# A decoder block on one core: products of four up-projection steps made ahead and kept in DRAM, a gain row applied to results, weight sums in other stages, half of a transposition inside w_out

## Chip, cores and metric

The kernel runs on one core of a Trainium2 chip. The metric is the device time of one execution in microseconds (us); where several runs are given, the median counts. Every time of the kernel before that is quoted from a trace comes from one profiled execution.

## What is computed

Batch 1, 1024 tokens, model width 1024, feed-forward width 2816 (22 blocks of 128, called j), everything in float32. The part that the change touches comes after the two attention branches:

```
y = sigmoid(g_mla) * (o_mla @ w_o_mla) + sigmoid(g_fox) * (o_fox @ w_o_fox)   # "mix"
x = x + g_m * (y @ w_out)                                                     # "w_out"
h = rmsnorm(x, norm_ffn_g) * (1 + sc_f) + sh_f
u = h @ w_up                                                                  # "ffn_up"
gate, val = causal depthwise conv of width 3 over u, split in two halves
x = x + g_f * ((silu(gate) * val) @ w_down)                                   # "w_down"
return rmsnorm(x, norm_final_g)
```

`g_m`, `sc_f`, `sh_f`, `g_f` are rows of 1024 that are computed from a conditioning vector `c`.

## The kernel before

Each float32 product is made of three matmuls (`mm3`, lines 99 to 101): an operand is split into a high part (a copy to a shorter format, on ScalarE = ACT, line 80) and a low part (the difference, on VectorE = DVE, line 89, or on GpSimd = POOL, line 92). The usual matmul is 128x128 by 128x512.

A list scheduler decides the order of the instructions of each engine when the kernel is built; the engine then executes them in that order. All DMAs are issued by SyncE (SP), also in order: a DMA whose buffer is not free, or whose data is not made, holds back all that stand behind it. Pools with a number of buffers (`wr` has 2, `up`'s `u` has 6, PSUM's `mm` 5 and `sd` 3) decide how far loads run ahead.

The stages, with their place in the profiled execution:

- Projections and attention, to about 759 us.
- **mix** (759 to 850): a loop over eight blocks `d` of 128 columns, 48 matmuls each. For a block, 2 x 256 KB of weights (`wr`) and two gates of 512 KB (`o_raw`) are loaded. Behind the loop the conv weights are loaded and turned.
- **w_out** (853 to 963): output tiles of 128 tokens x 512 columns. Three groups of four tiles, each group over all eight k; a fourth group tile by tile. For each group 4 loads of 512 KB bring the weights into `wr`. POOL multiplies each 512 columns by the gain row `gm` (line 1129), then ACT and DVE split them into `wx_w`. Between groups one and two the rows `gf` and `sf` are made (`late_row`, lines 308 to 312). In group three the first four token blocks are normalised and turned by TensorE (`first_chunk`).
- **second chunk** (963 to 978): the last four token blocks t = 4 to 7 are turned; for each, DVE makes sums and differences and splits them (`t_N`, `t_T`, `t_B`).
- **ffn_up** (978 to 1422): w_up by Strassen-Winograd, 7 products of 12 matmuls for each j. Two of the products of j = 0 and 1 (B11, B21) are made ahead and stay in PSUM; the product that continues from B11 starts from a "seed", a PSUM copy made by ACT (line 1185). In the same loop `load_right` brings 22 blocks of w_down (512 KB each), and `sum_right` (lines 1294 to 1297) makes the four combinations N1, T2, N3, N4 of each pair, four DVE operations and four stores of 256 KB. `stored` makes four sums of each pair of activations on POOL.
- **w_down** (1422 to 1643): 7 products over 6 entries of the stored combinations, from a ring of 5 loads.

Of the kernel before, what the change touches and what calls it, by code (L numbers as in the profile page):

```python
# [13 lines left out]
ALU = mybir.AluOpType  # L14
# [15 lines left out]
RIGHT = ("N1", "N3", "T2", "N4")  # L30
# [40 lines left out]
class Block:  # L71
# [82 lines left out]
    def scratch(self):  # L154
        d = self.dram
        self.d_rope = d([2, P, S], F32, "rope")
        self.d_krope = d([32, 2, S], F32, "krope")
        self.d_qx = d([8, 4, S], F32, "qx")
        self.d_kx = d([8, 4, S], F32, "kx")
        self.d_mq = [d([P, 2, S], F32, f"mq{p}") for p in range(4)]  # L160
        self.d_mr = [d([P, 2, S], F32, f"mr{p}") for p in range(2)]
        self.d_mk = [d([P, 2, S], F32, f"mk{p}") for p in range(4)]
        self.d_v = [d([P, NT, 8, P], F32, f"v{b}") for b in range(2)]
        self.d_gate = [d([P, S], F32, f"gate{k}") for k in range(16)]
        self.d_o = [d([P, S], F32, f"o{k}") for k in range(8)]
# [3 lines left out]
        self.d_left = {n: [d([P, len(e), 512], F32, f"{n}{e[0]}") for e in ENTRIES] for n in LEFT}  # L169
        self.d_right = {n: [d([P, len(e), 512], F32, f"{n}{e[0]}") for e in ENTRIES] for n in RIGHT}  # L170
# [774 lines left out]


    def mix_and_up(self):
        nc, tc, a, ps = self.nc, self.tc, self.a, self.ps
        self.cwp = Pool(tc, "cw", "left")
        yp = Pool(tc, "y", "left")  # L950
        gm = yp([P, D], F32, "gm")
        y = [[yp([P, KD, 512], R32, f"y{c}{h}") for h in range(2)] for c in range(2)]
        op, oh, ol = self.op, self.oh, self.ol
        for d in range(KD):
# [28 lines left out]
        rows = self.wr([P, 1024], F32, "wr", 2)[: 2 * NJ, :512].rearrange("j (w p) -> j w p", w=4)  # L983
        self.dma(rows[:, 0:3, :], a["conv_w"][0].rearrange("w (j p) -> j w p", p=P))
        self.dma(rows[:, 3, :], a["conv_b"][0].rearrange("(j p) -> j p", p=P))
        self.cw = self.cwp([P, 4, 2 * NJ], F32, "cw")
        pt = ps([P, 512], F32, "mm", 5)
        for i in range(4):
            nc.tensor.transpose(pt[:, i * 44 : (i + 1) * 44], rows[:, i, :], self.ident[:44, :44])
        nc.vector.tensor_copy(self.cw, pt[:, :176].rearrange("p (w j) -> p w j", w=4))  # L990
# [9 lines left out]
        groups = [(half, slice(n * 512, (n + 1) * 512)) for half in range(2) for n in range(2)]  # L1000
        todo = [(g, k) for g in range(4) for k in range(0, KD, 2)]
        ahead = []

        def load():
            if todo:
                g, k = todo.pop(0)
                ns = groups[g][1]
                ahead.extend(self.scaled_rows(a["w_out"], k, ns, gm[:, ns], lambda: (lambda w: (w[:, 0:512], w[:, 512:1024]))(wx([P, 1024], R32, "w", 9))))

        def residual(x, acc, ns):  # L1010
            nc.vector.tensor_tensor(out=x[:, ns], in0=acc, in1=x[:, ns], op=ALU.add)

        def modulated(t, x):
# [6 lines left out]
            (nc.gpsimd if t in (1, 3, 5) else nc.vector).tensor_tensor(out=h, in0=h, in1=sf, op=ALU.add)  # L1020
# [17 lines left out]
        load()  # L1038
        hs, xs = [], []
        for g, (half, ns) in enumerate(groups[:3]):  # L1040
# [3 lines left out]
            acc = [ps([P, 512], F32, *(("sd", 3) if g != 1 and i < 3 else ("mm", 5))) for i in range(4)]  # L1044
            for k in range(KD):
                if k in (0, KD - 2):
                    held = []
                if k % 2 == 0:
                    load()
                held.append(ahead.pop(0))  # L1050
                if k in (0, KD - 2):
                    continue
                for i in range(4):
                    ts = slice(i * P, (i + 1) * P)
                    for e, (hi, lo) in enumerate(held, k + 1 - len(held)):
# [16 lines left out]
        for _ in range(3):  # L1072
            load()
# [35 lines left out]
        first = []  # L1109
        operands = [self.gate_operands(j) for j in range(2)]  # L1110
        for t in range(4, 8):
            second_chunk(t, hs[t])
        for j in range(2):
            x1 = ps([P, 512], F32, "mm", 5)
            self.product(x1, operands[j][1], "B11", True)
            first.append(([None] + operands[j][1:], x1, self.seed(x1, -1.0)))
        for j in range(2):
            self.product(first[j][1], operands[j][2], "B21", False)
        gx.close()
        self.ffn_up(first, tp)  # L1120

    def scaled_rows(self, w_dram, k, cols, gain, room):
# [4 lines left out]
        for i in range(2):  # L1127
            x = w[:, i, :]
            self.nc.gpsimd.tensor_tensor(out=x, in0=x, in1=gain, op=ALU.mult)  # L1129
            hi, lo = room()  # L1130
            self.hi_act(hi, x)
            self.lo_dve(lo, x, hi)
            out.append((hi, lo))
# [69 lines left out]
    def ffn_up(self, first, tp):  # L1203
# [13 lines left out]
        self.load_right(0)  # L1217
        ahead = self.operands(0, first[0][0])
        for j in range(NJ):
            a11, a12, a22, s1, s2, s3, s4 = ahead  # L1220
            if j + 1 < NJ:
                ahead = self.operands(j + 1, first[j + 1][0] if j + 1 < len(first) else self.gate_operands(j + 1))
            if j < len(first):
                _, x1, x6 = first[j]
            else:
                x1 = bank()
                self.product(x1, a11, "B11", True)
                x6 = self.seed(x1, -1.0)
# [5 lines left out]
            if j % 2 and j < NJ - 1:  # L1234
                self.load_right((j + 1) // 2)
            ug, uv = up([P, S], F32, "u", 6), up([P, S], F32, "u", 6)
            if j >= len(first):
                self.product(x1, a12, "B21", False)
            copied(x1, ug[:, lower])
# [15 lines left out]
            if j % 2 == 0:  # L1255
                self.sum_right(j // 2)
# [8 lines left out]
    def stored(self, j, act):  # L1265
# [7 lines left out]
        even, G = self.even, self.nc.gpsimd.tensor_tensor  # L1273
# [7 lines left out]
        for n, y in (("S1", x[:, lower]), ("S3", x[:, upper]), ("S2", even[:, lower]), ("S4", act[:, lower])):  # L1281
            self.dma(self.place(n, m), y)

    def load_right(self, m):

        self.pair = [self.upp([P, D], F32, f"dw{i}") for i in range(2)]
        for i, w in enumerate(self.pair):
            self.dma(w, self.a["w_down"][0, (2 * m + i) * P : (2 * m + i + 1) * P, :])

    def sum_right(self, m):  # L1290

        V, (x, z) = self.nc.vector.tensor_tensor, self.pair
# [29 lines left out]
    def down_raw(self, p, i):  # L1322
# [3 lines left out]
        x, w = (ring([P, 2, 512], F32, t, 5)[:, : len(e), :] for t in ("ar", "br"))  # L1326
        self.dma(x, self.d_left[left][i])
        if right in RIGHT:
            self.dma(w, self.d_right[right][i])
        else:  # L1330
            blocks = self.a["w_down"][0].rearrange("(m e p) n -> e p m n", e=2, p=P)
            self.dma(w, blocks[int(right[1]) - 1][:, e[0] : e[-1] + 1, HALVES[int(right[2]) - 1]])
        return x, w

    def down_split(self):

        out = []
        for src, c in zip(self.coming.pop(0), "ab"):
# [163 lines left out]
```

## Time and profile before

| | us |
|---|---|
| median of 3 runs | 1647.35 |
| the runs | 1647.15, 1647.35, 1649.14 |
| profiled execution | 1645.47 |
| its span, first to last instruction | 1643.5 |
| PE (TensorE) busy | 1557.2 |
| DVE busy | 1100.9 |

The profiled execution lies 1.88 us under the median, and 1.97 us of it lie outside the span. An engine's busy time is a sum over stages; where it waits is read stage by stage. The granted TensorE clock is a share of full speed: 1.00 is 2.4 GHz, 0.50 is 1.2 GHz.

### The profile page before, as it was taken

The page shows a single profiled execution, that of the slowest core. Times are in us where ns is not written, and L with a number is a line of the kernel's source. Part 1 is how long each engine was busy: PE and PEld are TensorE (multiplying, and loading weights), DVE is VectorE, ACT ScalarE, POOL GpSimd, SP SyncE. Part 2 cuts the span into 40 slices and gives each one's busy share as a digit, 9 for nine tenths or more (in the row PEclk, how much of TensorE's full clock was granted, in tenths as well). Part 3 has the DMA queues.
Part 4 walks back from the last instruction along what each step waited for, and adds up shares of the span by engine and source line. Part 5 has one row for each costly group of instructions (what it writes and reads, how often), then busy time and mean ns, then how long its engine had stood idle before and what let it go on. Part 6 is the DMA issues. An engine that isn't in the chain of part 4 may idle for free.

```text
span 1643.5 us, 21193 instructions
## 1 busy us (share of the span) xinstructions
PE 1557.2 (95%) x7574; PEld 1279.1 (78%) x7574; DVE 1100.9 (67%) x1726; ACT 776.8 (47%) x1341; POOL 430.6 (26%) x366
## 2 busy tenths in 40 slices
PE   7899979999997999999998979999999999999997
PEld 3778868888886888887876757777778888888886
DVE  5755666566554566575655789988898767746467
ACT  3434345544444455465533446544455455535445
POOL 1322025676770322301226431111111111101010
PEclk9999999999998999999999979999999999999999
DMA  8435497767455534516434525565653333587652
GB/s 289 143 103 173 154 256 190 219 185 203 138 157 138 127 96 116 126 55 218 156 128 161 172 77 179 193 198 198 199 167 109 109 116 108 180 327 244 201 182 103
DMA packets 191414, 270.84 MB, mean 165 GB/s; under 512 B 13026, under 2 KB 112034, under 8 KB 189966
## 3 DMA queue, kind: packets, MB, share of 16 engines
q1 hardware_dynamic: 191310, 269.50, 52.1%
q8 instruction: 59, 0.97, 0.2%
q14 instruction: 45, 0.37, 0.1%
HBM read 183.21 MB, written 73.67 MB: 156 GB/s over the span
## 4 chain that ended last, share of the span: by engine, by line
PE 37%; DVE 7%; DMA 5%; issue 4%; POOL 2%; ACT 1%; SPq 0%; DVEq 0%; POOLq 0%; ACTq 0%
PE ps_mm L99 5%; PE ps_mm L100 5%; PE ps_mm L101 5%; PE ps_sd L99 3%; PE ps_sd L100 3%; PE ps_sd L101 3%; PE ps_x L100 2%; PE ps_x L101 2%; PE ps_x L99 2%; DVE up_u L1201 2%; PE ps_y L101 2%; PE ps_y L99 2%; PE ps_y L100 2%; DMA up_dw<-in_w_down_dram 1%; POOL wr_wr L1129 1%
## 5 line engine op out<-in xcount | busy, mean ns | idle before, releaser
L99 PE MATMUL psA_fill<-hT_hi,ws_wh 128*128 128x512 f32 x352 | 150.0, 426 | 0.0
L92 POOL TENSOR_TENSOR ws_wl<-wr_wr,ws_wh 128x512 fp32r<-128x512 f32 x62 | 82.6, 1334 | 229.3 <-ACT ws_wh L80 206.4
L755 ACT ACTIVATE att_p<-psA_s,small_soft 128x128 f32<-128x128 f32 (+7 forms) x128 | 94.7, 740 | 100.1 <-DVE small_soft L749 98.5
L101 PE MATMUL psA_fill<-hT_hi,ws_wl 128*128 128x512 f32 x352 | 139.4, 396 | 0.0
L100 PE MATMUL psA_fill<-hT_lo,ws_wh 128*128 128x512 f32 x352 | 139.3, 396 | 0.0
L749 DVE TENSOR_REDUCE small_soft<-psA_s 128x1 f32<-128x128 f32 (+7 forms) x128 | 96.0, 751 | 52.2 <-PE psA_s L747 51.8
L745 PE MATMUL psA_s<-opn_k,opn_q 96*128 96x256 f32 (+7 forms) x480 | 115.2, 360 | 16.0 <-DMA opn_k<-opn_stg 8.8
L1201 DVE SCALAR_TENSOR_TENSOR up_u<-up_u,cw_cw,up_u 128x1023 f32<-128x1023 f32 x88 | 110.7, 1277 | 1.8 <-ACT up_u L1199 1.6
L745 PEld LDWEIGHTS psA_s<-opn_k,opn_q 96*128 96x128 f32 (+1 forms) x480 | 82.4, 193 | 25.4 <-issue 15.5
L89 DVE TENSOR_TENSOR ring_al<-ring_ar,ring_ah 128x1024 fp32r<-128x1024 f32 (+1 forms) x41 | 49.5, 1207 | 65.5 <-ACT ring_ah L80 65.5
L89 DVE TENSOR_TENSOR att_ptl<-psA_pt,att_pth 128x512 fp32r<-128x512 f32 x96 | 66.0, 688 | 35.8 <-ACT att_pth L80 35.4
L774 PE MATMUL psA_pt<-const_ident,att_p 128*128 128x128 f32 x576 | 86.6, 273 | 0.0
L757 DVE TENSOR_SCALAR att_p<-att_p,small_soft 128x128 f32<-128x128 f32 (+7 forms) x128 | 82.1, 642 | 4.1
L80 ACT ACTIVATE ring_ah<-ring_ar 128x1024 fp32r<-128x1024 f32 (+1 forms) x41 | 40.4, 985 | 86.0 <-PE ps_x L100 58.0
L101 PEld LDWEIGHTS psA_fill<-hT_hi,ws_wl 128*128 128x128 f32 x352 | 66.4, 189 | 15.7
L286 POOL TENSOR_TENSOR att_acc<-att_acc,att_lw 128x512 f32<-128x512 f32 x56 | 74.5, 1331 | 4.3
L1199 ACT ACTIVATE up_u<-up_u,cw_cw 128x1024 f32<-128x1024 f32 x44 | 54.7, 1243 | 43.4 <-DVE up_u L1243 42.3
L99 PEld LDWEIGHTS psA_fill<-hT_hi,ws_wh 128*128 128x128 f32 x352 | 67.4, 191 | 9.6
L100 PEld LDWEIGHTS psA_fill<-hT_lo,ws_wh 128*128 128x128 f32 x352 | 66.9, 190 | 9.7
L99 PE MATMUL ps_mm<-h_b,uw_gh 128*128 128x512 f32 x176 | 70.7, 402 | 3.0 <-DVE t_B L89 3.0
L100 PE MATMUL ps_mm<-h_b,uw_gh 128*128 128x512 f32 x176 | 70.7, 402 | 0.0
L101 PE MATMUL ps_mm<-h_b,uw_gl 128*128 128x512 f32 x176 | 70.6, 401 | 0.0
(432 smaller groups left out, 4533.4 us busy)
## 6 DMA issues: line engine op xcount, KB each, us to landing
wr_wr<-in_w_up_dram SPq DMA_DIRECT2D x46, 512.0 KB
att_lw<-in_w_ada_dram SPq DMA_DIRECT2D x64, 256.0 KB
wr_wr<-in_w_in_dram SPq DMA_DIRECT2D x28, 512.0 KB
up_dw<-in_w_down_dram SPq DMA_DIRECT2D x22, 512.0 KB
dram_S<-up_u SPq DMA_DIRECT2D x44, 256.0 KB
ring_ar<-dram_S SPq DMA_DIRECT2D x20, 512.0 KB
dram_N<-up_dw SPq DMA_DIRECT2D x33, 256.0 KB
dram_A<-up_u SPq DMA_DIRECT2D x33, 256.0 KB
```

The costliest lines, as they stand in the source:

```text
L89: self.nc.vector.tensor_tensor(out=out, in0=in_, in1=f32(hi), op=ALU.subtract)
L92: self.nc.gpsimd.tensor_tensor(out=out, in0=in_, in1=f32(hi), op=ALU.subtract)
L99: mm(ps, lhsT=lh, rhs=rh, start=start, stop=False, skip_group_check=onto)
L100: mm(ps, lhsT=lh, rhs=rl, start=False, stop=False, skip_group_check=onto)
L101: mm(ps, lhsT=ll, rhs=rh, start=False, stop=stop, skip_group_check=onto)
L286: nc.gpsimd.tensor_tensor(out=acc, in0=acc, in1=w, op=ALU.add)
L745: mm(o, lhsT=l, rhs=r[:, keys], start=n_ == 0, stop=diag is None and n_ == len(passes) - 1)
L749: nc.vector.tensor_reduce(out=st[:, 0:1], in_=view(s), axis=AX.X if i < 4 else AX.XY, op=ALU.max, negate=True)
L755: nc.scalar.activation(po, view(s), AF.Exp, bias=st[:, 0:1], accum_out=st[:, 1:2])
L757: nc.vector.tensor_scalar(out=pr, in0=pr, scalar1=st[:, 2:3], scalar2=None, op0=ALU.mult)
L774: nc.tensor.transpose(pt[:, n * 256 + e * P : n * 256 + (e + 1) * P], pr[:, kb * P : (kb + 1) * P], self.ident)
L1201: nc.vector.scalar_tensor_tensor(out=dst[:, back:], in0=u[:, : S - back], scalar=cw[:, tap, jj : jj + 1], in1=dst[:, back:], op0=ALU.mult, ...
```

## The change

RIGHT, the set of w_down combinations kept in DRAM, shrinks from four to two (N1, T2). They are summed inside the mix loop: 11 times a load of 512 KB and one of 256 KB, two DVE operations, two stores of 256 KB. N3 and N4 are formed in w_down from an extra load and one DVE subtraction (12 times). The conv weights move into the mix loop (d = 4). In w_out the 32 POOL multiplications by `gm` go; instead DVE multiplies each of the 16 result tiles in PSUM. The groups run (0,0), (0,1), (1,1), (1,0), so that group three reuses the split weights of group two: 12 loads and 24 splits instead of 16 and 32. The turning of blocks 4 and 5 is placed inside w_out's last tile. The two early products are made for four j instead of two; their results are copied by ACT, stored in DRAM (`d_early`, 8 stores of 256 KB) and loaded again (8 loads). In `stored` the sums of j < 8 go from POOL to DVE.

```diff
-RIGHT = ("N1", "N3", "T2", "N4")
+RIGHT = ("N1", "T2")
+EARLY = 4
...
+    def load_right(self, pool, m):
+        x, z = pool([P, D], F32, "dx", 2), pool([P, 512], F32, "dz", 2)
+        self.dma(x, self.a["w_down"][0, 2 * m * P : (2 * m + 1) * P, :])
+        self.dma(z, self.a["w_down"][0, (2 * m + 1) * P : (2 * m + 2) * P, 512:1024])
+        return m, x, z
...
+    def sum_right(self, pool, d):
...
+        for m, x, z in self.blocks:
+            V(out=x[:, lower], in0=x[:, lower], in1=x[:, upper], op=ALU.subtract)
+            V(out=z, in0=z, in1=x[:, lower], op=ALU.add)
+            self.dma(self.place("N1", m), x[:, lower])
+            self.dma(self.place("T2", m), z)
+        self.blocks = [self.load_right(pool, self.unsummed.pop(0)) for _ in range(2 if 0 < d < 5 else d < 7)]
...
+            if d == 4:
+                self.conv_weights()
+            self.sum_right(op, d)
...
-        groups = [(half, slice(n * 512, (n + 1) * 512)) for half in range(2) for n in range(2)]
-        todo = [(g, k) for g in range(4) for k in range(0, KD, 2)]
+        groups = [(half, HALVES[n]) for half, n in ((0, 0), (0, 1), (1, 1), (1, 0))]
+        todo = [(n, k) for n in (0, 1, 0) for k in range(0, KD, 2)]
...
         def residual(x, acc, ns):
+            nc.vector.tensor_tensor(out=acc, in0=acc, in1=gm[:, ns], op=ALU.mult)
             nc.vector.tensor_tensor(out=x[:, ns], in0=acc, in1=x[:, ns], op=ALU.add)
...
-                if g == 2 and k in (2, 3, 4, 5):
-                    first_chunk(k - 2, hs[k - 2])
+                if g == 2 and k in (3, 4, 5, 7):
+                    t = min(k - 3, 3)
+                    first_chunk(t, hs[t])
...
+        def early(j, left, right):
+            if right == "B11":
+                banks[j] = ps([P, 512], F32, "sd", 3)
+            self.product(banks[j], left, right, right == "B11")
+            x = gx([P, 512], F32, "e", 2)
+            nc.scalar.activation(x, banks[j], AF.Copy)
+            self.dma(self.d_early[j][:, int(right == "B21"), :], x)
...
+        with tc.high_priority(400):
+            second_chunk(4, hs[4])
+            second_chunk(5, hs[5])
...
-            self.nc.gpsimd.tensor_tensor(out=x, in0=x, in1=gain, op=ALU.mult)
...
+        def first_product(j):
+            if j < EARLY:
+                x = up([P, 512], F32, "p1", 2)
+                self.dma(x, self.d_early[j][:, 0, :])
+                return x
...
+            x6 = self.seed(x1, -1.0)
...
-            if j % 2 == 0:
-                self.sum_right(j // 2)
...
-        even, G = self.even, self.nc.gpsimd.tensor_tensor
+        even, G = self.even, (self.nc.vector if j < 8 else self.nc.gpsimd).tensor_tensor
...
+        if minus is not None:
+            self.nc.vector.tensor_tensor(out=w, in0=w, in1=minus, op=ALU.subtract)
```

The first place is SP's row in the mix: before, weights (`wr`) and gates only.

```order
405 L77 DMA o_raw_7910<-dram_gate_18_101 128x1024
406 L77 DMA o_raw_7913<-dram_gate_26_109 128x1024
407 L77 DMA wr_wr_8071<-in_w_o_mla_dram 128x4x128
408 L77 DMA wr_wr_8071<-in_w_o_fox_dram 128x4x128
409 L77 DMA wr_wr_8163<-in_w_o_mla_dram 128x4x128
410 L77 DMA o_raw_7978<-dram_acc_46_129 128x1024
411 L77 DMA wr_wr_8163<-in_w_o_fox_dram 128x4x128
```

In the changed kernel, at the same place, `dx` and `dz` are the blocks of w_down, `dram_N` and `dram_T` the stores of their sums.

```order
417 L79 DMA dram_T_108_191<-o_dz_7979 128x512
418 L79 DMA wr_wr_8095<-in_w_o_mla_dram 128x4x128
419 L79 DMA o_raw_8011<-dram_gate_19_102 128x1024
420 L79 DMA dram_row_130<-y_gm_7811 1x1024
421 L79 DMA o_raw_8014<-dram_gate_27_110 128x1024
422 L79 DMA dram_N_103_186<-o_dx_7982 128x512
423 L79 DMA dram_T_109_192<-o_dz_7983 128x512
424 L79 DMA o_dx_8087<-in_w_down_dram 128x1024
425 L79 DMA o_dz_8088<-in_w_down_dram 128x512
426 L79 DMA o_dx_8091<-in_w_down_dram 128x1024
427 L79 DMA o_dz_8092<-in_w_down_dram 128x512
428 L79 DMA wr_wr_8095<-in_w_o_fox_dram 128x4x128
```

The weights of block d = 3 (`wr_wr_8071` before, `wr_wr_8095` now) stood at places 407 and 408 and now stand at 418 and 428, with five blocks of sums loaded and three of them stored ahead of them.

The second place is ACT in w_out, where the row `sf` is made between the first and the second group; `wx_w` are high parts of w_out weights. Before:

```order
691 L80 ACTIVATE wx_w_8732<-wr_wr_8729 128x512
692 L80 ACTIVATE wx_w_8736<-wr_wr_8729 128x512
693 L80 ACTIVATE wx_w_8766<-wr_wr_8763 128x512
694 L80 ACTIVATE wx_w_8770<-wr_wr_8763 128x512
695 L312 ACTIVATE gx_sf_8500<-ps_mm_8671 128x512
696 L312 ACTIVATE gx_sf_8500<-ps_mm_8675 128x512
697 L80 ACTIVATE wx_w_8800<-wr_wr_8797 128x512
```

And now:

```order
692 L82 ACTIVATE wx_w_8782<-wr_wr_8777 128x512
693 L82 ACTIVATE wx_w_8811<-wr_wr_8809 128x512
694 L82 ACTIVATE wx_w_8814<-wr_wr_8809 128x512
695 L82 ACTIVATE wx_w_8979<-wr_wr_8977 128x512
696 L315 ACTIVATE gx_sf_8580<-ps_mm_8749 128x512
697 L315 ACTIVATE gx_sf_8580<-ps_mm_8753 128x512
698 L1047 ACTIVATE gx_h_8898,small_ss_8899<-gx_x_8757 128x1024
```

The splits still stand ahead of `gx_sf`, but no POOL operation stands ahead of the splits any more.

The third place is SP at the entry of ffn_up in the changed kernel; `gx_e` are copies of early products, `up_p` the loads from which the first two seeds are made. Before, neither existed.

```order
518 L79 DMA dram_early_100_183<-gx_e_9546 128x512
519 L79 DMA dram_early_101_184<-gx_e_9562 128x512
520 L79 DMA dram_early_100_183<-gx_e_9577 128x512
521 L79 DMA dram_early_101_184<-gx_e_9592 128x512
522 L79 DMA up_p_1_9624<-dram_early_98_181 128x512
523 L79 DMA up_p_2_9648<-dram_early_99_182 128x512
524 L79 DMA up_u_9681<-dram_early_98_181 128x512
```

The load of the first seed's data stands behind the store of the last early product.

## Rows read from the trace of the kernel before

**Rows 1.** The page: the span, and part 1 for TensorE (busy, share, instructions).
```profile
span 1643.5 us, 21193 instructions
PE 1557.2 (95%) x7574; PEld 1279.1 (78%) x7574; DVE 1100.9 (67%) x1726; ACT 776.8 (47%) x1341; POOL 430.6 (26%) x366
```

**Rows 2.** Windows: us, busy PE, PEld, DVE, ACT, POOL, clock, DMA share, GB/s.
```profile
1200.00:1225.00 25.00, 25.00 (x111) 20.42 (x110) 22.02 (x22) 12.17 (x15) 5.65 (x4) 1.00 0.63 211
1250.00:1275.00 25.00, 25.00 (x111) 20.42 (x110) 19.72 (x22) 13.07 (x16) 1.29 (x1) 1.00 0.30 91
1450.00:1475.00 25.00, 25.00 (x112) 20.68 (x111) 10.73 (x10) 11.05 (x14) 0.00 (x0) 1.00 0.95 357
```

**Rows 3.** What TensorE waited for, 849 to 1225 us: total, times, longest.
```profile
PE ps_mm L99 <- DVE gx_gf L310: 6.3, 1, 6.3
PE ps_sd L99 <- ACT ps_sd L1185: 5.6, 3, 2.1
PE ps_mm L1027 <- DVE t_B L89: 5.4, 1, 5.4
PE ps_sd L99 <- DVE up_u L1241: 3.9, 3, 1.7
PE ps_mm L1027 <- DVE gx_x L1101: 3.7, 1, 3.7
PE ps_mm L1027 <- DVE h_b L89: 3.5, 1, 3.5
PE ps_mm L99 <- DVE t_B L89: 3.0, 1, 3.0
PE ps_sd L99 <- ACT wx_w L80: 2.4, 1, 2.4
PE ps_sd L99 <- ACT uw_sh L80: 1.1, 1, 1.1
PE ps_sd L99 <- ACT up_c L1214: 0.8, 1, 0.8
PE ps_mm L99 <- ACT uw_sh L80: 0.8, 1, 0.8
```

**Rows 4.** Windows of 10 us in mix, w_out and the second chunk, same columns.
```profile
770.00:780.00 10.00, 10.00 (x46) 8.24 (x45) 7.60 (x11) 5.47 (x8) 1.91 (x2) 1.00 0.78 247
880.00:890.00 10.00, 5.32 (x18) 4.31 (x19) 6.63 (x7) 2.86 (x5) 7.07 (x6) 0.66 0.62 225
930.00:940.00 10.00, 9.39 (x38) 7.69 (x39) 8.28 (x13) 5.92 (x12) 2.54 (x2) 0.83 0.29 90
970.00:980.00 10.00, 3.85 (x12) 2.85 (x13) 10.00 (x15) 5.34 (x10) 3.20 (x3) 0.50 0.00 0
```

**Rows 5.** Timelines of POOL, ACT and DVE, 876 to 885 us: start, length, instruction.
```profile
876.71 5.85 POOL L1129 TENSOR_TENSOR wr_wr<-wr_wr,y_gm 128x512 f32<-128x512 f32 x4 [2.54 <-DMA wr_wr<-in_w_out_dram]
882.59 0.63 ACT L80 ACTIVATE wx_w<-wr_wr 128x512 fp32r<-128x512 f32 x1 [1.04 <-POOL wr_wr L1129]
883.12 1.06 ACT L312 ACTIVATE gx_sf<-ps_mm 128x512 f32<-128x512 f32 x2
883.86 1.28 DVE L310 SCALAR_TENSOR_TENSOR gx_gf<-ps_mm,gx_gf 128x512 f32<-128x512 f32 x2
```

**Rows 6.** SP's timeline in the mix, DMA of 755 to 850, POOL's weight splits.
```profile
763.96 5.86 SPq L77 DMA_DIRECT2D o_raw<-dram_gate  x4
DMA packets 8992, 15.06 MB, mean 158 GB/s; under 512 B 567, under 2 KB 5863, under 8 KB 8986
L92 POOL TENSOR_TENSOR ws_wl<-wr_wr,ws_wh 128x512 fp32r<-128x512 f32 x62 | 82.6, 1334 | 229.3 <-ACT ws_wh L80 206.4
```

**Rows 7.** The tile of w_down's sums: one operation (min/median/max ns), and why DVE idled.
```profile
L1296 DVE TENSOR_TENSOR up_dw<-up_dw,up_dw x11: 680/1668/1677, 996.9 to 1221.9; 128x512 f32<-128x512 f32 x11
  DMA up_dw<-in_w_down_dram: 12.9, 4
  issue: 9.1, 3
```

More of the change, by code (lines that the diff above doesn't have):

```diff
@@ L169, in scratch @@
         self.d_left = {n: [d([P, len(e), 512], F32, f"{n}{e[0]}") for e in ENTRIES] for n in LEFT}
+        self.d_early = [d([P, 2, 512], F32, f"early{j}") for j in range(EARLY)]
         self.d_right = {n: [d([P, len(e), 512], F32, f"{n}{e[0]}") for e in ENTRIES] for n in RIGHT}
@@ L950, in mix_and_up @@
         yp = Pool(tc, "y", "left")
+        y = [[yp([P, KD, 512], R32, f"y{c}{h}") for h in range(2)] for c in range(2)]
         gm = yp([P, D], F32, "gm")
-        y = [[yp([P, KD, 512], R32, f"y{c}{h}") for h in range(2)] for c in range(2)]
         op, oh, ol = self.op, self.oh, self.ol
+        self.blocks, self.unsummed = [], list(range(NJ // 2))
         for d in range(KD):
@@ L1036, in first_chunk @@
                 self.lo_dve(b1[1][sl], v, b1[0][sl])
-        load()
+        for _ in range(2):
+            load()
         hs, xs = [], []
@@ L1044, in mix_and_up @@
             acc = [ps([P, 512], F32, *(("sd", 3) if g != 1 and i < 3 else ("mm", 5))) for i in range(4)]
+            weights = []
             for k in range(KD):
-                if k in (0, KD - 2):
-                    held = []
-                if k % 2 == 0:
+                if k % 2 == 0 and g < 2 and (g, k) < (1, 4):
                     load()
-                held.append(ahead.pop(0))
+                weights.append((kept if g == 2 else ahead).pop(0))
                 if k in (0, KD - 2):
                     continue
+                first = k - 1 if k in (1, KD - 1) else k
                 for i in range(4):
                     ts = slice(i * P, (i + 1) * P)
-                    for e, (hi, lo) in enumerate(held, k + 1 - len(held)):
-                        self.mm3(acc[i], y[half][0][:, e, ts], y[half][1][:, e, ts], hi, lo, e == 0, e == KD - 1)
-                held = []
-                if g == 2 and k in (2, 3, 4, 5):
-                    first_chunk(k - 2, hs[k - 2])
+                    for e in range(first, k + 1):
+                        self.mm3(acc[i], y[half][0][:, e, ts], y[half][1][:, e, ts], *weights[e], e == 0, e == KD - 1)
+                if g == 2 and k % 2:
+                    load()
+                if g == 2 and k in (3, 4, 5, 7):
+                    t = min(k - 3, 3)
+                    first_chunk(t, hs[t])
+            kept = weights
             if g == 0:
@@ L1107, in second_chunk, with split_rows @@
                 (self.lo_pool if n == "N4" else self.lo_dve)(lo, v[n], hi)
[L1109 to L1112, printed above, removed]
+        def early(j, left, right):
[5 more added lines that the diff above has]
+            self.dma(self.d_early[j][:, int(right == "B21"), :], x)
+        banks = {}
+        gates = [self.gate_operands(j) for j in range(2)]
+        with tc.high_priority(400):
+            second_chunk(4, hs[4])
+            second_chunk(5, hs[5])
         for j in range(2):
-            x1 = ps([P, 512], F32, "mm", 5)
-            self.product(x1, operands[j][1], "B11", True)
-            first.append(([None] + operands[j][1:], x1, self.seed(x1, -1.0)))
+            early(j, gates[j][1], "B11")
+        second_chunk(6, hs[6])
         for j in range(2):
-            self.product(first[j][1], operands[j][2], "B21", False)
+            early(j, gates[j][2], "B21")
+        gates += [self.gate_operands(j) for j in range(2, EARLY)]
+        second_chunk(7, hs[7])
+        for j in range(2, EARLY):
+            early(j, gates[j][1], "B11")
+        for j in range(2, EARLY):
+            early(j, gates[j][2], "B21")
         gx.close()
-        self.ffn_up(first, tp)
-    def scaled_rows(self, w_dram, k, cols, gain, room):
+        self.ffn_up(tp)
+    def split_rows(self, w_dram, k, cols, room):
         w = self.wr([P, 1024], F32, "wr", 2).rearrange("p (i n) -> p i n", i=2)
@@ L1233, in ffn_up @@
             t = copied(x6)
-            if j % 2 and j < NJ - 1:
-                self.load_right((j + 1) // 2)
             ug, uv = up([P, S], F32, "u", 6), up([P, S], F32, "u", 6)
-            if j >= len(first):
+            if j < EARLY:
+                self.dma(ug[:, lower], self.d_early[j][:, 1, :])
+            else:
                 self.product(x1, a12, "B21", False)
-            copied(x1, ug[:, lower])
+                copied(x1, ug[:, lower])
             self.product(x6, s3, "N3", False)
```

85 lines of the change are left out of this document (39 added, 46 removed).

## The prediction, made before the changed kernel ran

> **What bounds the kernel now.** I read the page first: TensorE is busy for 1557.2 of 1643.5 us [rows 1], so a change that leaves the count of matmuls as it is (the order has 6763 rows on PE before and 6764 after) can save at most some 86 us of idle time, plus what the lower clock costs. Next, the 25-us windows: where TensorE never waits it does 111 or 112 matmuls in 25 us, 0.223 us each [rows 2]. Then what TensorE waited for between the mix and the middle of ffn_up [rows 3]: eleven kinds of wait, 36.5 us in all. Six of them lie in w_out and the turning of the second chunk (2.4 + 6.3 + 3.5 + 3.7 + 5.4 + 3.0 = 24.3 us), the others (12.2 us) at the entry of ffn_up and in its first half. In the mix it does not wait: 10.00 us busy in 770 to 780 [rows 4], and so it goes on in that stage; in w_down there is hardly a wait either (25.00 of 25 in 1450 to 1475 [rows 2]). So the change can win in w_out, the second chunk and ffn_up's first half, and it can lose in the mix, to which it moves work, and in w_down.
>
> After a wait the clock is lower: 0.66, 0.83 and 0.50 as means over the three 10-us windows that hold the waits for `gx_gf`, `h_b` and the second chunk [rows 4]. These are mixes of the levels 2.4 and 1.2 GHz: 0.66 is 6.8 us of ten at the lower one. If these lay last in the wait and first behind it, some 2.7 us fell on work behind the first wait and cost half of it, 1.3 us; by the same way 1.5 us behind the second.
>
> **The mix (loss).** 11 blocks x (512 + 256 KB loaded, 2 x 256 KB stored) are 14.4 MB, beside 15.06 MB that moved there before, at 158 GB/s on average [rows 6]. The 22 DVE operations of about 0.68 us (the shortest of `up_dw` [rows 7]) are 15 us in a stage where DVE is busy for 7.6 of 10 us at its fullest [rows 4], which is room enough over 91 us. The danger is SP: block d = 3's weights now stand behind five blocks of sums, d = 4's behind more. Counting the sizes of SP's new row from the first gate load (issued at 764 us [rows 6]), 9.7 MB lie up to and with d = 3's weights, 14.4 up to d = 4's, 18.7 to d = 5's, 22.1 to d = 6's. TensorE needs them at 793, 805, 816 and 827 us (the stage's 759 to 850 in eight equal blocks), about 3 us after landing: two splits on POOL of 1.33 each [rows 6]. With a rate r the lateness for d = 5 is 764 + 18.7 MB / r + 3 - 816. The highest rate in the trace is 357 GB/s at a DMA share of 0.95 [rows 2], 376 at a full share; 770 to 780 us had 247 at 0.78 [rows 4], 317 at a full share. At 376 d = 5 is 1 us late, at 340 6, at 300 13. I take 340, between the best row and the nearest scaled one: **+6 us**, with bounds 0 and +13.
>
> By the Trainium skill (HBM Reference, Specifications) a core that streams alone reaches about 425 GB/s. No run here shows it: the trace's best is 357. By that page the term would be 0, and the case would be the second rival's below.
>
> **w_out (gain).** The 6.3 us go to `gf` and `sf` [rows 3]. The timelines show why [rows 5]: POOL multiplies four tiles in 5.85 us after 2.54 us of waiting for a load, ACT splits the last at 882.59, only then turns to `gx_sf` (883.12), and DVE to `gx_gf` (883.86). ACT's order keeps splits ahead of `gx_sf` in the changed kernel, but these wait for loads alone; two loads are ahead instead of one. With 1.46 us of POOL per tile gone, I let TensorE resume about 0.6 us after its own last matmul for that row: 6.3 - 0.6 + 1.3 of clock is **-7 us**. The 3.5 us wait for `h_b` was DVE held up by weight splits and long operations beside POOL; in the new order group three needs no new splits and the turns come one k later. The gain is 3.5 + 1.5 of clock; I keep 1 us of it as a rest, **-4 us**. The first wait (2.4, ACT busy with the end of the mix) stays. DVE gets 16 products of about 0.7 us and loses 8 splits of the same length: +5.5 us, in a stage where it is not full. Bounds for w_out: -12 (both waits and their clocks gone) and -4 (the wait for `gf` only halved).
>
> **Second chunk and entry of ffn_up (even).** Before, 12.1 us of waits and about 2 us of lower clock. In 970 to 980 us DVE is busy for all 10 us [rows 4]: it is the limit there, with four blocks of sums and splits, and these stay. Turning two of them inside the last w_out tile saves perhaps 2.5 us, since the other two still wait for the residual and the norm. The next 48 matmuls made early are 10.7 us [rows 2], in which DVE prepares ffn_up's operands. But the first seed now comes from DRAM: last copy on ACT, store, load behind it on SP, then the seed. A load for which POOL waited took over 2.54 us [rows 5]; store and load one after the other are some 5 us, from the end of the early products, against 1.9 us of entry waits before [rows 3]. -2.5 + 3.1 is about 0: **0 us**, bounds -4 and +5.
>
> **ffn_up (gain).** Of its 12.2 us of waits 1.9 are the entry's, which leaves 10.3 [rows 3], on `ps_sd` seeds (ACT) and `up_u` (DVE). They come behind stretches where DVE stood still in front of `up_dw`: 12.9 us for w_down's loads and 9.1 by issue [rows 7]; DVE is in order, so all of ffn_up's own work stands behind it. With the sums gone these stop; 1200 to 1225 has DVE at 22.0 of 25 us with the sums, and 1250 to 1275, without them, at 19.7 with no wait on TensorE [rows 2]. Against that: j = 0 to 3 have five products, 60 matmuls or 13.4 us, and DVE needs at most 14.7 there: per j its row has seven operations on 512 columns, seven on 1024, and four sums of `stored` for every second j, at 0.64 us for 512 columns back to back (1.28 for two [rows 5]). DVE lags by up to 1.3 us per j, 5 in all, of which the buffers take some: I keep 4 us of waits. **-6.3 us**, bounds -9 and -2. `stored`'s sums on DVE last only to j = 7.
>
> **w_down (nothing).** 12 subtractions of about 1.3 us (twice 0.64) and 5.8 MB more. In 1450 to 1475 DMA is at 0.95, but the extra loads belong to products five to seven, later, and DVE is busy for 10.7 of 25 us there [rows 2]. Hidden by the ring's lookahead; without that cover, up to +3.
>
> **Sum.** +6 - 7 - 4 + 0 - 6.3 + 0 = -11.3 us on the profiled execution's 1645.47: 1634.2. The median of the runs lies 1.9 above it, so 1636.0 us.
>
> **Rivals.**
>
> *The mix starves (slower).* SP's queue is in order, and the new `dx` loads wait for their buffers' stores, so the stream stops and starts, as the mean of 158 GB/s shows it doing now [rows 6]. It decides when the mix loses 20.6 us, that is, by 17.3 us of other gains and the 3.3 us of the 0.2%: 18.7 MB in 816 + 20.6 - 767 = 69.6 us, a sustained 269 GB/s. For it: 247 in 770 to 780 [rows 4]. Against it: that window's share was 0.78, with SP's loads not wanted sooner. Time: at 250 GB/s d = 5 is 26 us late, 1656 us. Chance 0.17.
>
> *The mix hides everything (faster still).* At 376 GB/s or more the term is 0 to 1 and the entry wait overlaps: 1636 - 5 - 3 = 1628 us. For it: the highest row; against it: stores and loads wait for one another. Chance 0.19.
>
> *The waits only move (no change).* The `gf` and `sf` row stays behind splits whose loads come late, and DVE, with 16 more products in w_out and sums of `stored`, gives up half of ffn_up's gain: -3.5 - 2 - 3 + 6 = -2.5, 1645 us. For it: ACT's row keeps four splits ahead of `sf`; DVE is near full in the first half of ffn_up [rows 2]. Against it: DVE's idle time there is blocked time, not lack of work [rows 7]. Chance 0.14.
>
> The forecast itself: 0.50, with its own range 1630 to 1643.
>
> **Numbers.** 0.2% is 3.3 us, about what a measurement tells from no change; 1644.1 to 1650.6 counts as the same. Faster: 0.50 + 0.19 = 0.69, of which 0.01 goes to the upper edge: 0.68. Same: 0.14 and that 0.01: 0.15. Slower: 0.17. The range leaves out half of the starving case and the edge of the fast one: 1625 to 1652.
>
> **What would show it.** Mix: TensorE waits for `wr` splits at d = 3 to 6, 5 to 7 us in all, with the DMA share over 0.9 between 764 and 820 us. w_out: no wait over 2 us for `gx_gf`, none for `h_b`, clock at 1.00 there. Second chunk: waits for `t_B` or `uw_gl`, then one of about 5 us for the seed from DRAM. ffn_up: no idle DVE in front of loads, about 4 us of waits in j = 0 to 4, none behind j = 8. w_down: no new wait. It is wrong if the mix is longer than 101 us, if the seeds on ACT, which run ahead in order and wait for the `p1` loads, hold up the copies that free PSUM, or if DVE's lag in j = 0 to 3 is paid in full.

## The result, and the profile after

| | before | changed |
|---|---|---|
| median of 4 runs, us | 1647.25 | 1630.41 |
| lowest and highest | 1644.00 to 1649.14 | 1626.37 to 1634.27 |
| profiled execution | 1645.47 | 1631.67 |
| its span | 1643.5 | 1629.9 |

The ratio is 0.990, with a 95% interval of 0.987 to 0.9929: the change is faster by 12 to 21 us. Forecast were 11.3 us and a median of 1636.0, with a range of 1630 to 1643; the measured median lies 0.4 us inside the range's lower end. The two profiled executions differ by 13.8 us, and the stages are compared on them. The page after, against [rows 1]:

```profile
span 1629.9 us, 21135 instructions
...
PE 1552.7 (95%) x7574; PEld 1274.8 (78%) x7574; DVE 1086.5 (67%) x1741; ACT 776.4 (48%) x1337; POOL 356.8 (22%) x317
```

What TensorE waited for in the changed kernel, 745 to 1225 us, against [rows 3] (total us, times, longest):

```profile
PE ps_mm L311 <- ACT o_raw L82: 7.0, 2, 5.6
PE ps_sd L103 <- DVE uw_gl L91: 4.3, 1, 4.3
PE ps_mm L1057 <- DVE gx_h L1050: 2.8, 2, 2.5
PE ps_sd L101 <- ACT wx_w L82: 2.7, 1, 2.7
PE ps_sd L101 <- ACT uw_sh L82: 2.5, 1, 2.5
PE ps_mm L101 <- ACT uw_sh L82: 2.2, 1, 2.2
PE ps_mm L1057 <- DVE t_B L91: 1.8, 1, 1.8
PE ps_mm L103 <- DVE uw_sl L91: 0.7, 1, 0.7
PE ps_mm L102 <- DVE o_ol L91: 0.5, 1, 0.5
PE ps_sd L101 <- ACT ws_wh L82: 0.5, 1, 0.5
PE ps_sd L101 <- ACT up_c L1259: 0.4, 1, 0.4
PE ps_sd L103 <- POOL ws_wl L94: 0.4, 1, 0.4
PE ps_sd L101 <- DVE up_u L1293: 0.4, 1, 0.4
...
```

The waits for `gx_gf` (6.3) and `h_b` (3.5) are gone, and of the 10.3 us in ffn_up the last rows of this list are left, 1.5 us (`uw_sl`, `up_c`, `up_u`). At the head stands a wait that the kernel before does not have: TensorE at line 311, the matmuls of a late row, in the mix. The clock and the stages are read in 10-us windows (columns as in [rows 2]; the first three lie in the mix, then w_out's `gf`/`sf` place, then the second chunk):

```profile
770.00:780.00 10.00, 10.00 (x46) 8.26 (x45) 9.23 (x15) 5.12 (x7) 1.77 (x2) 1.00 0.84 299
...
800.00:810.00 10.00, 7.71 (x32) 5.42 (x30) 5.76 (x10) 3.38 (x4) 1.27 (x1) 1.00 0.92 330
810.00:820.00 10.00, 5.78 (x16) 4.19 (x17) 4.34 (x6) 5.83 (x8) 3.03 (x2) 0.66 0.96 337
...
880.00:890.00 10.00, 9.83 (x44) 7.81 (x43) 7.47 (x13) 4.32 (x8) 0.00 (x0) 1.00 0.50 164
...
960.00:970.00 10.00, 3.74 (x14) 2.22 (x12) 9.66 (x14) 8.32 (x14) 3.53 (x3) 0.83 0.01 2
970.00:980.00 10.00, 7.60 (x27) 6.12 (x28) 10.00 (x17) 5.45 (x10) 4.97 (x3) 0.83 0.58 184
```

880 to 890, where [rows 4] had 5.32 us of TensorE at a clock of 0.66, now has 9.83 at 1.00. In exchange 810 to 820 lies at 0.66 with DMA at 0.96 of its time.

Where a stage begins is read from the rows of the tiles, the first start of a group of matmuls:

```profile
L101 PE MATMUL ps_mm<-o_oh,ws_wh x64: 387/389/628, 759.3 to 858.3; 128*128 128x512 f32 x64
...
L103 PE MATMUL ps_mm<-wx_w,y_y x80: 388/389/398, 869.3 to 959.9; 128*128 128x512 f32 x80
L101 PE MATMUL ps_sd<-wx_w,y_y x48: 389/389/499, 864.5 to 933.0; 128*128 128x512 f32 x48
...
L101 PE MATMUL ps_sd<-t_T,uw_sh x88: 389/389/793, 1001.8 to 1396.8; 128*128 128x512 f32 x88
...
L101 PE MATMUL ps_x<-uw_gh x8: 389/389/389, 1408.5 to 1413.2; 128*128 128x512 f32 x8
```

The mix runs from the first row's first start to the third's, w_out from there to the second's last start, the turning with the early products to the fourth's first start (the first seeded product), ffn_up to the fifth's, w_down to the span's end. The same rows in every run give this table (us):

| kernel | mix | w_out | turn, early | ffn_up | w_down | median | ratio, 95% interval |
|---|---|---|---|---|---|---|---|
| before | 93.8 | 107.4 | 34.3 | 427.6 | 221.4 | 1647.25 | |
| changed | 105.2 | 95.4 | 41.9 | 406.7 | 221.4 | 1630.41 | 0.990 (0.987 to 0.9929) |
| changed, again (e11) | 106.8 | 96.6 | 42.8 | 407.0 | 221.4 | 1632.14 | 0.9908 (0.9888 to 0.9929) |
| e1 row later | 106.5 | 96.5 | 42.9 | 407.2 | 221.4 | 1633.33 | 0.9915 (0.9896 to 0.9935) |
| e2 sums in ffn_up | 95.4 | 96.6 | 44.7 | 410.1 | 221.3 | 1626.53 | 0.9876 (0.9854 to 0.9899) |
| e3 POOL scales | 107.9 | 104.2 | 42.0 | 407.0 | 221.6 | 1638.64 | 0.9965 (0.995 to 0.9979) |
| e4 two j early | 105.7 | 96.6 | 36.5 | 415.5 | 221.6 | 1634.25 | 0.9922 (0.9904 to 0.9939) |
| e5 `stored` on POOL | 109.5 | 95.0 | 42.3 | 408.4 | 221.4 | 1637.67 | 0.9949 (0.993 to 0.9968) |
| e6 turn behind w_out | 105.8 | 94.1 | 46.2 | 407.0 | 221.4 | 1631.56 | 0.9916 (0.9886 to 0.9947) |
| e7 paced sums | 95.5 | 95.0 | 43.6 | 407.1 | 221.4 | 1623.57 | 0.986 (0.9835 to 0.9885) |
| e8 before, two sums | 94.3 | 108.9 | 34.2 | 423.5 | 221.3 | 1641.28 | 0.9972 (0.996 to 0.9983) |
| e9 four buffers | 112.3 | 96.5 | 43.0 | 407.1 | 221.4 | 1639.97 | 0.997 (0.9956 to 0.9984) |
| e10 paced, six early | 96.3 | 96.6 | 55.0 | 397.5 | 221.9 | 1628.29 | 0.9888 (0.9873 to 0.9904) |

Two columns belong together: of two more j made early, 48 matmuls (10.7 us) go from ffn_up to the column before it. The changed kernel and its repetition show how far a stage differs by itself: 1.6 us in the mix, 1.2 in w_out, 0.9 in the turning, 0.3 in ffn_up. The mix of all kernels that sum 11 blocks in it with two buffers lies between 105.2 and 109.5, and the changed kernel's profiled execution has the shortest of these. Differences of an experiment are therefore given against both executions of the changed kernel where it matters. Where the mix begins differs too, from 754.3 to 760.7 us, in stages that no edit touches; this is why stages are compared, and not spans.

Against before the changed kernel's profiled execution stands thus: mix +11.4, w_out -12.0, turning and early products +7.6 less 10.7 = -3.1, ffn_up -20.9 plus 10.7 = -10.2, w_down 0. Each of these rests on one profiled execution of either kernel; with e11 in its place the first three are +13.0, -10.8 and -2.2.

### The profile page after: what moved, and what is told of

Same layout as the page of the kernel before. It is cut to its first block, busy times and chain, and to the rows that moved or that the text cites. A ratio compares the mean times of both kernels' runs of the same rounds, so it can differ in the third digit from the quotient of the medians.

```text
span 1629.9 us, 21135 instructions
## 1 busy us (share of the span) xinstructions
PE 1552.7 (95%) x7574; PEld 1274.8 (78%) x7574; DVE 1086.5 (67%) x1741; ACT 776.4 (48%) x1337; POOL 356.8 (22%) x317
## 4 chain that ended last, share of the span: by engine, by line
PE 43%; DVE 4%; DMA 4%; ACT 2%; issue 1%; SPq 0%; ACTq 0%; DVEq 0%
PE ps_mm L101 5%; PE ps_mm L103 5%; PE ps_mm L102 5%; PE ps_sd L101 4%; PE ps_sd L103 4%; PE ps_sd L102 4%; PE ps_x L102 2%; PE ps_x L103 2%; PE ps_x L101 2%; PE ps_y L102 2%; PE ps_y L101 2%; PE ps_y L103 2%; DMA wr_wr<-in_w_up_dram 1%; DVE up_u L1246 1%; DMA o_raw<-dram_acc 1%
## 5 line engine op out<-in xcount | busy, mean ns | idle before, releaser
L760 DVE TENSOR_SCALAR att_p<-att_p,small_soft 128x128 f32<-128x128 f32 (+7 forms) x128 | 86.1, 672 | 4.1
L82 ACT ACTIVATE uw_sh<-uw_s 128x1024 fp32r<-128x1024 f32 x44 | 46.7, 1062 | 61.8 <-PE ps_mm L102 29.2
L91 DVE TENSOR_TENSOR uw_gl<-wr_wr,uw_gh 128x1024 fp32r<-128x1024 f32 x24 | 29.5, 1232 | 65.9 <-ACT uw_gh L82 64.4
L1328 POOL TENSOR_TENSOR up_u<-up_u 128x512 f32<-128x512 f32 x7 | 9.0, 1288 | 263.9 <-DVE up_u L1306 263.9
L82 ACT ACTIVATE att_pth<-psA_pt 128x512 fp32r<-128x512 f32 x96 | 57.2, 595 | 19.8 <-PE psA_pt L777 16.2
```

The lines of the kernel that those rows point to most:

```text
L82: self.nc.scalar.activation(out, in_, AF.Copy, scale=scale)
L91: self.nc.vector.tensor_tensor(out=out, in0=in_, in1=f32(hi), op=ALU.subtract)
L760: nc.vector.tensor_scalar(out=pr, in0=pr, scalar1=st[:, 2:3], scalar2=None, op0=ALU.mult)
```

## The experiments

**e1: is it the row's place, or the transfers?** In the changed kernel ACT got the row's vector at 813.08 only. Timelines of SP, ACT and TensorE of the changed kernel:

```profile
806.68 0.42 SPq L79 DMA_DIRECT2D o_raw<-dram_acc  x1
813.08 1.06 ACT L82 ACTIVATE o_raw<-o_raw 128x1024 fp32r<-128x1024 f32 x1 [1.88 <-DMA o_raw<-dram_acc]
814.18 1.22 PE L311 MATMUL ps_mm<-o_raw,const_ones 128*128 128x512 f32 x2 [5.58 <-ACT o_raw L82]
```

```diff
-            for late, g in ((1, 5), (3, 2)):
+            for late, g in ((1, 5), (6, 2)):
```

> The changed kernel with the second late row (g_m) made at d = 6 instead of d = 3; nothing else. Theory A, queue order: in the changed mix the weights are in time but for 0.9 us, and TensorE stands 5.6 us at the row's matmuls because the 512-KB load of its vector is behind sums' loads on SP. Then the wait goes, w_out begins about 7 us earlier (the wait and the half-speed stretch behind it), near 857.5 instead of 864.5, and no other wait of the mix grows beyond 1 us. Theory B, transfer rate: DMA is full from 790 to 840 us, and whatever comes last is waited for; then the weights of d = 4 and 5 are late instead, and w_out begins at most 2 us earlier, at 862 or later.

Measured: the mix took 106.5 us, as before the edit (105.2 and 106.8). The rows' wait fell from 7.0 to 1.7 us, and in its place stood another, in the same window and at the same lower clock (0.66 in 810 to 820):

```profile
PE ps_mm L101 <- ACT ws_wh L82: 4.8, 1, 4.8
```

Theory A fell: the row was only the first to arrive late.

**e2: the sums out of the mix again.** `sum_right` and `load_right` are called in the loop of ffn_up, once for every second j:

```diff
-            self.sum_right(op, d)
...
+            if j % 2 and j < NJ - 1:
+                pair = self.load_right(up, (j + 1) // 2)
...
+            if j % 2 == 0:
+                self.sum_right([pair])
```

> The changed kernel with the sums N1 and T2 taken out of the mix and made in the feed-forward up stage again, one pair of loads for every second j, two operations each instead of four; one buffer each for w_down's blocks and for the reloaded early products, since the pool has no room for two. Theory A (the prediction's): loads that the in-order vector engine waits for cost the up stage its stalls; then some 5 to 9 us of waits come back between its first seed and its end (the changed kernel has 1.5 us there), while the mix gets 11.5 us shorter; the whole is about even with the changed kernel, -6 to 0 us. Theory B: the up stage's gain came from the lighter vector engine (two operations fewer per j, their weight and time halved here); then at most 3 us of waits come back and the whole is 8 to 12 us faster than the changed kernel.

Measured: mix 95.4, which is 9.8 less; ffn_up 410.1, 3.4 more; the turning 2.8 more, where the buffers' number had to change too. TensorE's waits in ffn_up came to 6.9 us, 5.4 more than in the changed kernel, and the median is 3.9 us below the changed kernel's: both lie in the bounds of theory A. The stage grew by less than its waits did; why is open. Moving the sums won less in ffn_up than it cost in the mix. In ffn_up DVE still stood in front of these blocks, but a fifth of [rows 7]'s 22.0 us:

```profile
L973 DVE TENSOR_TENSOR up_dx<-up_dx x11: 675/684/693, 992.4 to 1181.9; 128x512 f32<-128x512 f32 x11
...
  DMA up_dx<-in_w_down_dram: 4.5, 2
```

**e3: POOL scales the weights again.**

```diff
-            nc.vector.tensor_tensor(out=acc, in0=acc, in1=gm[:, ns], op=ALU.mult)
...
+            self.nc.gpsimd.tensor_tensor(out=w[:, i, :], in0=w[:, i, :], in1=gain, op=ALU.mult)
```

> The changed kernel with w_out's weights multiplied by the gain row on GpSimd again and the 16 multiplications of results taken out; the new order of the groups, the 12 loads and the two loads ahead stay. Theory A (the prediction's): the wait for the shift and scale rows comes from splits paced by GpSimd; then a wait of 4 to 7 us with a half-speed stretch comes back between groups one and two, and w_out (first matmul to the last tile) is 6 to 10 us longer than the 95.6 us of the changed kernel. Theory B: the second load ahead and the reused weights removed it; then w_out grows by less than 3 us.

Measured: w_out 104.2, 8.8 longer (7.6 against e11). Theory A holds: the wait is back, and with it the lower clock in its window:

```profile
PE ps_mm L101 <- DVE gx_gf L313: 6.7, 1, 6.7
```

```profile
890.00:900.00 10.00, 5.14 (x12) 4.11 (x13) 6.71 (x7) 2.92 (x6) 7.32 (x6) 0.53 0.63 219
```

The wait for `h_b` is not back; the reused weights and the later turns, which stayed, go with its end. The two were not taken apart.

**e4: early products for two j.**

```diff
-EARLY = 4
+EARLY = 2
```

> The changed kernel with early products for two j instead of four, still stored in DRAM and loaded again. Theory A (the prediction's): making more products early moves work and gains nothing; then the total is within 3 us of the changed kernel, the entry wait longer by about what the 48 matmuls no longer cover. Theory B: the 48 matmuls fill time in which TensorE would have waited for operands at the entry; then the waits at the entry grow from 4.7 us to 10 us or more, and the total is 5 to 10 us longer.

Measured: 36.5 + 415.5 against 41.9 + 406.7, so 3.4 us more, and 2.2 more against e11's 42.8 + 407.0. That lies at the edge of theory A's 3 us and below theory B's 5 to 10; the entry's waits grew from 4.7 to 9.1 us (8.3 here and 0.8 at the first seed), near theory B's 10. So the 48 matmuls do fill a wait, but are worth less than theory B held:

```profile
PE ps_mm L101 <- ACT uw_sh L82: 8.3, 1, 8.3
```

In ffn_up alone two j are the better number: 415.5 - 10.7 = 404.8 against 406.7. A likely reason is that DVE cannot quite follow in a five-product j; no run shows it apart.

**e5: `stored` on POOL for all j.**

```diff
-        even, G = self.even, (self.nc.vector if j < 8 else self.nc.gpsimd).tensor_tensor
+        even, G = self.even, self.nc.gpsimd.tensor_tensor
```

> The changed kernel with the four sums of `stored` on GpSimd for all j, as before. Theory A: the vector engine is full in j = 0 to 7 and each operation moved to it costs there, so with 16 operations less on it the up stage (first seed product to the first matmul of w_down, 406.7 us in the changed kernel) gets 1 to 3 us shorter. Theory B: GpSimd's operations lengthen the vector engine's while they run (0.68 us to 1.67 in the trace of the kernel before), so moving them away was part of the up stage's gain; then the stage gets 2 to 6 us longer.

Measured: ffn_up 408.4, 1.7 longer; theory A fell, and B's bound was not reached. The longest `uw_sl` split of 1000 to 1170 us took 1994 ns, in the changed kernel 1226; the median of the 20 splits is nearly the same (1224 and 1217). By the Trainium skill (SBUF — State Buffer, Who interferes with whom) a DVE operation with two SBUF inputs contends with a POOL operation that reads SBUF. That split, with a POOL operation of `stored` running beside it, and the doubled operations of [rows 7] agree. Of the 6.0 us between the two profiled executions 4.3 lie in the mix, 109.5 us, which the edit does not touch.

**e6: blocks 4 and 5 left to the scheduler.**

```diff
-        with tc.high_priority(400):
-            second_chunk(4, hs[4])
-            second_chunk(5, hs[5])
+        second_chunk(4, hs[4])
+        second_chunk(5, hs[5])
```

> The changed kernel without the raised priority of blocks 4 and 5, so that the scheduler is free to turn them behind w_out's last tile. Theory A (the prediction's 2.5 us): from the end of the last tile to the first seed product TensorE then takes 2 to 4 us more than the changed kernel's 41.9 us, and the total is 1 to 3 us longer once the 2.4 us of turning that leave w_out are counted. Theory B: the vector engine's work sets that stretch and is the same in both, so the total stays within 1 us.

Measured: w_out 94.1, turning 46.2, together 140.3 us. That is 3.0 us more than the changed kernel's 137.3, but 0.9 more than e11's 139.4, which is the same kernel; the medians, 1631.56 against 1630.41 and 1632.14, do not differ either. The run does not separate the two theories, and the prediction's 2.5 us are neither shown nor refuted.

**e8: the halved sums alone, in the kernel before.** (`down_raw` and `down_split` as in the change.)

```diff
-RIGHT = ("N1", "N3", "T2", "N4")
+RIGHT = ("N1", "T2")
...
-        V(out=x[:, upper], in0=x[:, upper], in1=z[:, upper], op=ALU.subtract)
-        V(out=z[:, lower], in0=z[:, lower], in1=z[:, upper], op=ALU.subtract)
```

> The kernel before with one part of the change alone: N1 and T2 are summed in the up stage as before, N3 and N4 come from a subtraction in w_down with an extra load. The 22 loads of 512 KB stay. Theory A (loads that the vector engine waits for): the loads are the same, so most of the 10.3 us of waits in the up stage stay, at most 4 us go. Theory B (weight of the work): half of the sums are gone, and 6 to 9 us of the waits go. In both w_down stays at its length within 1 us, as in the changed kernel.

Measured: ffn_up 423.5, 4.1 less than before, w_down unchanged. Of the 10.3 us of TensorE's waits 7.3 stayed, as theory A had it. The issue part of DVE's standstill (9.1 in [rows 7]) went, most of that for the loads (12.9) stayed:

```profile
  DMA up_dw<-in_w_down_dram: 9.9, 4
```

**e7: paced sums.** One block per d, four in ffn_up, with 512 columns per load and a j between load and use (the added function `rest` subtracts, stores N1, loads the second block, adds, stores T2):

```diff
-        self.blocks = [self.load_right(pool, self.unsummed.pop(0)) for _ in range(2 if 0 < d < 5 else d < 7)]
+        self.blocks = [self.load_right(pool, self.unsummed.pop(0)) for _ in range(d < 7)]
...
+            if 8 <= j <= 16:
+                self.rest(up, j - 8)
```

> The changed kernel with the sums paced: one block per d in the mix (seven of eleven), the other four in the up stage at j = 8 to 16, in two tiles of 512 columns, each load placed a whole j ahead of its use. If the mix lost its 11.5 us to the transfer rate (14.4 MB more at about 335 GB/s), 9.2 MB more fit: the mix takes 94 to 96 us instead of 105.2, no wait in it over 0.6 us; the up stage keeps its 406 to 408 us, as the vector engine has 5 us of 25 free there; the total is 8 to 11 us below the changed kernel, 1619 to 1623. If the order of SP's queue and the wait for buffers cost the time, not the bytes, the mix stays above 100 us.

Measured: mix 95.5, ffn_up 407.1: both gains at once, and the lowest median of all, 1623.57, 0.986 of before (e2's interval overlaps with this one's). The total is 6.8 us below the changed kernel's, a little less than the 8 to 11 expected. The wait for the row fell to 1.1 us. Windows of this kernel's mix:

```profile
800.00:810.00 10.00, 10.00 (x46) 8.21 (x45) 7.09 (x9) 5.38 (x9) 4.30 (x3) 1.00 0.83 266
810.00:820.00 10.00, 10.00 (x47) 8.05 (x46) 7.50 (x12) 5.50 (x7) 1.30 (x2) 1.00 0.99 340
```

In the second window DMA is as full as in the changed kernel (0.99 and 0.96 of its time), and TensorE does not wait there. From 755 to 850 us 23.84 MB moved, in the changed kernel 28.82. The edit thus takes bytes out of the mix and spaces the rest, and the run does not say which of the two was needed: a kernel with all 11 blocks in the mix, evenly spaced, was not run.

**e9: four buffers for the blocks.**

```diff
-        x, z = pool([P, D], F32, "dx", 2), pool([P, 512], F32, "dz", 2)
+        x, z = pool([P, D], F32, "dx", 4), pool([P, 512], F32, "dz", 4)
```

> The changed kernel with four buffers instead of two for the blocks of w_down that are summed in the mix; the same bytes and the same operations. Theory A (transfer rate): DMA is at 0.91 to 1.02 of its time from 790 to 840 us, so letting loads be issued earlier only puts more of them ahead of the weights: the mix stays at 104 to 109 us or gets longer. Theory B (queue): SP waits some 33 us for sums and stores of these blocks while it holds the weights' loads back; with four buffers those waits go and the mix falls below 100 us.

Measured: 112.3 us, 7.1 more than the changed kernel and 2.8 above the longest mix with two buffers (109.5, e5). Theory B falls. DMA reached 365 GB/s from 800 to 810, and 160 in the next window:

```profile
800.00:810.00 10.00, 6.70 (x17) 5.01 (x18) 3.52 (x6) 3.90 (x5) 3.03 (x2) 0.66 1.06 365
810.00:820.00 10.00, 8.98 (x40) 7.05 (x38) 7.76 (x11) 2.48 (x4) 1.53 (x1) 1.00 0.49 160
```

The time is theory A's, but its reason does not show: in both kernels seven blocks of w_down were on the queue ahead of d = 4's weights, which were issued at 807.5 and 807.2 us, and the mean rate from 755 to 850 us fell to 283 GB/s. SP's waits for the blocks' stores shrank (`dram_N` from 12.2 to 2.0 us), but those for the sums' first operation grew as much (12.7 to 19.0), and from 814 to 820 us SP stood at the load of a gate until DVE had freed its buffer, part of this row:

```profile
SPq L79 <- DVE o_raw L1009: 8.1, 2, 5.9
```

The next weights were issued at 826.1 us, in the changed kernel at 820.7. So the in-order queue has its share, and more buffers do not remove it.

**e10 and e11: six j early on top of e7, and the changed kernel again.**

```diff
-EARLY = 4
+EARLY = 6
...
+        for pair in ((2, 3), (4, 5)):
```

> The kernel with paced sums and early products for six j instead of four. Theory A: the entry wait is already covered with four (4.7 us of waits are left there, behind operands that ACT and the vector engine make), and in j = 4 and 5 the vector engine needs more than the 13.4 us of 60 matmuls; the total is within 3 us of the paced kernel. Theory B: each further pair covers waits as the step from two to four did; then another 3 to 5 us go.

Measured: 55.0 + 397.5 against e7's 43.6 + 407.1, 1.8 us more. By these stages theory A holds, and two further j win nothing; the medians differ by 4.7 us, more than its 3. Of the 8.5 us between the two profiled executions 6.6 lie in stages that the edit does not touch.

> The changed kernel once more, beside the two others on one chip, to see how far a stage differs from run to run: the mix within 104 to 110 us, w_out within 94 to 97, from its last tile to the first seed product within 41 to 43, the up stage behind it within 406 to 409, w_down at 221.4.

Measured: all stages within these bounds (106.8, 96.6, 42.8, 407.0, 221.4).

## Why the prediction was right or wrong, point by point

**The mix, +6 predicted, +11.4 measured: mis-sized, and the late thing was another.** That the sums in the mix make what TensorE needs late holds: without them the stage is 95.4 us long (e2), and delaying one late consumer only uncovers the next (e1). The term that was mis-sized is the rate: I took 340 GB/s as if it lasted. The 10-us windows from 800 to 830 us have 330 to 337, but the stage as a whole, with the stretches in which SP waited for sums and buffers, moved less (DMA view of the changed kernel, 755 to 850 us):

```profile
DMA packets 14953, 28.82 MB, mean 303 GB/s; under 512 B 1235, under 2 KB 6531, under 8 KB 14947
```

With 303 my own formula gives 764 + 61.7 + 3 - 816 = 12.7, near what was measured; this rate is read from the very stage that it explains, so the agreement is no separate test. ACT split d = 4's weights here:

```profile
814.04 0.62 ACT L82 ACTIVATE ws_wh<-wr_wr 128x512 fp32r<-128x512 f32 x1
814.89 0.63 ACT L82 ACTIVATE ws_wh<-wr_wr 128x512 fp32r<-128x512 f32 x1 [0.22 <-DMA wr_wr<-in_w_o_fox_dram]
```

By the prediction's count 14.4 MB had then come since 764 us, 283 GB/s. How much of the loss is due to the bytes and how much to SP's standing still, no run takes apart. I also had the weights waited for at every d; the late row, which I did not count among those that hang on SP, took most of the wait in one piece (5.6 of 7.0 us), and the lower clock behind it (0.66 in 810 to 820) came on top. The DMA share that I expected, over 0.9 from 764 on, was reached from 790 on only; 770 to 780 had 0.84. My own mark, a mix over 101 us, was passed. The starving rival has the right place; its price of 26 us did not come.

**w_out, -11 predicted, -12.0 measured (-10.8 with e11).** With the turning of two blocks inside, some 2 us that stood behind it before, it is nearer -14. e3 shows that POOL's scaling held `gf`: the stage grew by 7.6 to 8.8 us with that scaling back, against 7 predicted for that wait. The 4 us for `h_b` were not tested by themselves. The DVE products cost nothing that shows: of TensorE's waits in w_out only the first (2.7) is over 0.3 us.

**Second chunk and entry, 0 predicted, -3.1 measured, about -1 without the 2 us that went into w_out.** The gain from turning two blocks early (predicted 2.5) stays open: e6 puts it at 0.9 to 3.0. The predicted price, 5 us for a seed from DRAM, does not show as a wait for the load: at that place TensorE waits 2.2 + 2.5 for `uw_sh`, against 1.9 before. A price that I did not count follows it: the granted clock of 1000 to 1010 us is 0.69, in the kernel before 1.00, which by these figures costs about 2 us (an estimate) and lies in ffn_up's column. And that the 48 early matmuls fill time in which operands are made I named, but gave no figure; by e4 it is worth 2.2 to 3.4 us net.

**ffn_up, -6.3 predicted, -10.2 measured: mis-sized.** I gave all of it to the standstill of DVE in front of the sums. That this standstill makes TensorE wait holds: 5.4 us of waits come back with the loads (e2), and 7.3 of 10.3 stay with them (e8). The single steps show three parts: half of the sums gone, 4.1 (e8); the rest moved to the mix, 3.4 (e2, which changes buffers too); `stored` on DVE, 1.7 (e5; 1.4 against e11), which I had counted as a cost. If they may be added, though each was measured in another kernel, they make 9.2; the price of two more five-product j, 1.9 by e4, lies on the other side, so 2.9 us of the 10.2 are not put down to any step. The term that was mis-sized is the 4 us of waits that I kept for j = 0 to 4: 1.5 us were measured.

**w_down, 0 predicted, 0 measured**, 221.4 in both. The extra loads (`ring_cr`) are issued from 1481 us on. In their fullest window, the second below, DMA moves 336 GB/s where the kernel before had 282, and TensorE does not wait; the stage's highest rate, in the first line, comes before them:

```profile
1425.00:1450.00 25.00, 25.00 (x112) 20.68 (x111) 12.43 (x12) 11.05 (x14) 0.00 (x0) 1.00 1.01 389
...
1500.00:1525.00 25.00, 25.00 (x112) 20.67 (x112) 14.13 (x13) 10.55 (x14) 0.00 (x0) 1.00 0.91 336
```

The total of 11.3 thus came out near the measured time in part by luck: the mix's missing 5 us and ffn_up's and the second chunk's 7 more stand against one another.

## What to carry to other kernels

Work moved into a stage with idle engines still pays for its bytes: divide all bytes due up to the next needed load by a rate below the best window's, since a stage pauses (here 303 GB/s on average, where its windows had up to 337), and count every consumer on the queue, not only the weights. When such a move lost, four buffers instead of two won nothing here (112.3 us against 105.2 to 109.5), while one block per step instead of two, with four of the eleven left to a later stage, kept the gains and gave back 9.7 us of the mix. Where an in-order engine waits for loads in the middle of its own work, halving those operations gave about as much (4.1 us) as moving the rest to another stage (3.4).

## What the runs showed of the hardware that was not expected

DMA moved 389 GB/s over 25 us at a share of 1.01, above the 376 that I had worked out as the full share from [rows 2]. By the Trainium skill (HBM Reference, Specifications) a core alone reaches about 425; no run shows that, but 389 lies nearer to it than the 357 of the kernel before. The mix did not come near it: its mean was 303, and even its windows with a DMA share over 0.9 had 303 to 337.
